# Attention of a two-layer decoder step: the low halves of four query weights are made by an adding transfer instead of a VectorE subtraction

## The chip, the cores and the metric

The kernel runs on one core of a Trainium2 chip. The time is device microseconds of the whole program, from one execution to the next the median of several runs. The profile is one execution taken by the hardware profiler; its engines are PE (TensorE, its matmuls) and PEld (its weight loads), DVE (VectorE), ACT (ScalarE), POOL (GpSimd) and SP (SyncE, which here only issues transfers).

## The reference, cut to what matters

One step of a decoder with two layers, all in float32: 512 new prompt positions and 8 sample rows (one new token each), model width 1024. Layer 0 mixes with sliding-window attention (16 query heads, 2 key/value heads, head size 64, window 128), layer 1 with gated linear attention; after each comes a ConvFFN of width 2816. The change touches only the first product of layer 0:

```python
qkv = x @ w_qkv + b_qkv                       # (520 x 1024) @ (1024 x 1280)
q, k = rope(q, pos), rope(k, pos)
scores = einsum('bnqkgd,bnskd->bnkgqs', qb, kk) * 64 ** -0.5
probs = sink_softmax(scores, mask, sink)      # softmax with one more logit per head
o = einsum('bnkgqs,bnskd->bnqkgd', probs, vv)
x = layer_norm(ALPHA * x + o @ w_o)           # then the ConvFFN, then layer 1
```

The outputs are compared with this in float32, so the kernel keeps the precision: each operand of a product is split into a high part that TensorE reads in its fast float32 form (`fp32r`) and a low part, the remainder.

## The kernel before, in words

**Units.** All weights are cut into units of 128 output columns; a unit is one array of 128 x 1024 float32 (512 KB). Units 0 and 1 are the key and value columns, units 2 to 9 the query columns (`attn_q`, two heads each), units 10 to 17 the output projection (`out_proj`), then the ConvFFN and layer 1 follow. The 520 rows of x are two groups: a (256 rows) and b (264 rows, the samples among them). Each unit is multiplied with both groups.

**A weight's way.** `load_unit` brings a unit from HBM by SP into a tile `raw` (2 buffers). ACT copies it to `wh` with rounding to `fp32r` (line 198); then DVE takes `wl = raw - wh` (line 204). `wh` and `wl` come from a pool of `WSLOTS` = 6 slots, so units 0 to 5 are loaded at the start and unit 6 takes the slot of unit 0 when both groups are done with that, unit 7 that of unit 1, and so on. For the units of the ConvFFN (`ffn_down2`, `ffn_gate`, `ffn_value`) another way is in use, `low_by_dma`: ACT writes `-wh` into `wl` (line 209), and a transfer that POOL issues reads the unit from HBM once more and adds it to `wl` while it writes (line 210).

**A product.** `product` makes, for each of 8 blocks of 128, three matmuls into one accumulator `accp`: `wh` by the high part of x (line 240), `wh` by its low part (242), `wl` by the high part (244). So 24 matmuls for a unit and a group, of which the third needs `wl`.

**Attention behind it.** `attn_q` takes each query product of a unit and a group as one task (16 of them): ACT reads `accp` (line 573, tile `ra`), DVE and POOL rotate it (575, 576, 577, 579, tile `rr`), ACT and DVE split it (624, 625, tile `hl`), SP moves the halves into place with 4 small transfers (629, tile `qs`); then come scores on PE (657 and 658, tile `sc`, in two halves of 4 matmuls), mask, maximum and exponential on DVE and ACT (667 to 677, the exponential is line 674), transposes on PE (686, tile `tp`), their copies on ACT (688) with POOL's two selections (692), and the products with the values on PE (705).

**What sets the order.** The program is written in one sequence, and a scheduler of the framework then orders each engine's instructions by its own cost model and puts the semaphores in. Each engine works through its own list strictly in that order. An instruction that waits holds up all that stand behind it on its engine. So a change of one operation's kind can move others that are not touched in the source.

Of the kernel before, what the change touches and what calls it, by code (L numbers as in the profile page):

```python
# [45 lines left out]
WSLOTS = 6  # L46
# [56 lines left out]
class Net:  # L103
# [80 lines left out]
    def load_unit(self, u, pieces=1, late=False):  # L184
        src, nt = self.units[u][0], self.units[u][1]
        nc = self.nc
        if nt == 0:
            return self.load_rank(u)
        r = self.raw.tile([P, KD * P], F32, name="raw")
        h, l = ((self.wx if u == self.extra else self.wts).tile([P, KD * P], F32R, name=name) for name in ("wh", "wl"))  # L190
        n = nt * P // pieces
        for c in (slice(i * n, (i + 1) * n) for i in range(pieces)):
            nc.sync.dma_start(out=r[:, c], in_=src[:, c])
            if late:
                self.spawn(self.parts(u, h[:, c], l[:, c], r[:, c], src[:, c]), 1)
                continue
            if u >= HIACT:
                nc.scalar.activation(h[:, c], r[:, c], AF.Copy)  # L198
            else:
                nc.gpsimd.tensor_scalar(h[:, c], r[:, c], 1.0, 0.0, op0=ALU.mult, op1=ALU.add)  # L200
            if self.units[u][2] in (self.ffn_down2, self.ffn_gate, self.ffn_value):
                self.low_by_dma(l[:, c], h[:, c], src[:, c])
            else:
                nc.vector.tensor_tensor(l[:, c], r[:, c], h[:, c].bitcast(F32), op=ALU.subtract)  # L204
        self.w[u] = (h, l)
# [1320 lines left out]
```

## Time and profile before

| | |
|---|---|
| median of 3 runs | 1097.23 us (1093.21 to 1097.97) |
| the profiled execution | 1098.08 us, of which 1096.1 us are the profile's span |
| granted TensorE clock, mean | 0.994 |
| PE matmuls busy | 1058.4 us, 97% of the span |
| DVE, ACT, POOL busy | 79%, 63%, 30% of the span |
| DMA | 167.44 MB, 153 GB/s on average |
| transfers by `low_by_dma` | 85 in the span, none of them issued before 153 us |

All times within the profile are in us from the start of the span. The attention of layer 0 lies between about 15 and 136 us; the profiled execution is 0.85 us above the median of the runs.

### The profile page before, as it was taken

To read this page: it belongs to the slowest core of one execution; us is meant where nothing else is said; L and a number is where in the kernel's file an instruction comes from. 1 tells how busy PE (TensorE), PEld (TensorE's weight loads), DVE (VectorE), ACT (ScalarE), POOL (GpSimd) and SP (SyncE) were. 2 spreads that over 40 slices of the span, in tenths; PEclk is the share of its full clock that TensorE was granted. 3 is DMA by queue.
4 is the path that set the end of the run, shared out by engine and by line. 5 is a ranking of instruction groups with operands and counts; after the bars stand their busy time and mean duration, and the time that the engine had idled before them with its cause. 6 is when DMAs were issued, how large, how long until landed. Compare 5 with 4: busy or idle time off the path is not lost.

```text
span 1096.1 us, 23852 instructions
## 1 busy us (share of the span) xinstructions
PE 1058.4 (97%) x9174; PEld 1029.8 (94%) x9174; DVE 866.2 (79%) x1812; ACT 686.1 (63%) x1356; POOL 325.8 (30%) x513
## 2 busy tenths in 40 slices
PE   8999999999999999999999999999899999999995
PEld 7998799999999999999999999898899999999995
DVE  7897758987788778978766767687888788778975
ACT  5677657776656665647666756477676656665643
POOL 3476553511111110274231111363311111110263
PEclk9999999999999999999999999999999999999998
DMA  6554139597777774348134455367487777774422
GB/s 228 150 162 136 24 108 226 129 221 183 181 174 175 174 190 117 111 144 220 55 115 157 132 157 172 93 173 209 127 212 187 181 173 177 174 188 117 114 68 79
DMA packets 65473, 167.44 MB, mean 153 GB/s; under 512 B 8104, under 2 KB 28624, under 8 KB 65360
## 3 DMA queue, kind: packets, MB, share of 16 engines
q1 hardware_dynamic: 50960, 119.47, 33.6%
q0 software_dynamic: 12240, 44.57, 23.2%
q10 hardware_dynamic: 2160, 1.89, 0.5%
q8 instruction: 72, 1.18, 0.4%
q14 instruction: 41, 0.34, 0.1%
HBM read 153.24 MB, written 8.47 MB: 148 GB/s over the span
## 4 chain that ended last, share of the span: by engine, by line
PE 76%; DVE 8%; DMA 6%; ACT 4%; POOL 2%; issue 2%; SPq 1%; DVEq 0%; ACTq 0%; POOLq 0%
PE widep L312 9%; PE widep L314 9%; PE widep L313 9%; PE accp L240 8%; PE accp L242 8%; PE accp L244 7%; PE widep L937 5%; PE widep L934 5%; PE widep L936 5%; DMA raw<-in_w_up 2%; PE accp L954 2%; DMA raw<-in_w_qkv 2%; PE onep L314 1%; PE onep L313 1%; PE onep L312 1%
## 5 line engine op out<-in xcount | busy, mean ns | idle before, releaser
L317 ACT ACTIVATE wh<-raw 128x1024 fp32r<-128x1024 f32 x72 | 76.3, 1060 | 96.2 <-PE widep L937 49.9
L198 ACT ACTIVATE wh<-raw 128x1024 fp32r<-128x1024 f32 (+1 forms) x91 | 95.0, 1047 | 40.7 <-PE widep L313 12.4
L313 PE MATMUL widep<-tl,wh 128*128 128x264 f32 (+1 forms) x432 | 119.1, 276 | 0.0
L314 PE MATMUL widep<-th,wl 128*128 128x264 f32 (+1 forms) x432 | 119.1, 276 | 0.0
L312 PE MATMUL widep<-th,wh 128*128 128x264 f32 (+1 forms) x432 | 119.1, 276 | 0.0
L240 PE MATMUL accp<-xh_b,wh 128*128 128x264 f32 x400 | 112.6, 282 | 2.5 <-DVE hprod L831 2.0
L244 PE MATMUL accp<-xh_b,wl 128*128 128x264 f32 x400 | 111.7, 280 | 0.0
L210 POOL DMA_DIRECT2D wl<-in_w_down x28 | 24.3, 866 | 284.2 <-ACT wl L209 273.1
L240 PE MATMUL accp<-xs_a,wh 128*128 128x256 f32 x400 | 105.6, 283 | 2.9 <-ACT wh L198 1.9
L242 PE MATMUL accp<-xl_b,wh 128*128 128x264 f32 x384 | 106.8, 278 | 0.0
L242 PE MATMUL accp<-xs_a,wh 128*128 128x256 f32 x384 | 102.1, 282 | 0.5 <-DVE xs_a L318 0.4
L318 DVE TENSOR_TENSOR wl<-raw,wh 128x1024 fp32r<-128x1024 f32 x72 | 88.1, 1223 | 8.1 <-ACT wh L317 8.1
L209 ACT ACTIVATE wl<-wh 128x1024 fp32r<-128x1024 f32 x85 | 89.3, 1053 | 1.1
L204 DVE TENSOR_TENSOR wl<-raw,wh 128x1024 fp32r<-128x1024 f32 (+2 forms) x63 | 77.9, 1244 | 14.0 <-ACT wh L198 13.4
L312 PEld LDWEIGHTS widep<-th,wh 128*128 128x128 f32 x432 | 82.1, 190 | 0.0
L313 PEld LDWEIGHTS widep<-tl,wh 128*128 128x128 f32 x432 | 82.1, 190 | 0.0
L314 PEld LDWEIGHTS widep<-th,wl 128*128 128x128 f32 x432 | 82.1, 190 | 0.0
L858 DVE TENSOR_TENSOR merged<-widep,conv 128x528 f32<-128x528 f32 x72 | 37.4, 561 | 55.3 <-PE widep L314 55.2
L240 PEld LDWEIGHTS accp<-xs_a,wh 128*128 128x128 f32 x400 | 76.4, 194 | 4.5 <-ACT wh L198 2.5
L312 PE MATMUL widep<-xh_b,wh 128*128 128x264 f32 x288 | 79.6, 276 | 0.0
L313 PE MATMUL widep<-xl_b,wh 128*128 128x264 f32 x288 | 79.5, 276 | 0.0
L314 PE MATMUL widep<-xh_b,wl 128*128 128x264 f32 x288 | 79.5, 276 | 0.0
(426 smaller groups left out, 4048.1 us busy)
## 6 DMA issues: line engine op xcount, KB each, us to landing
raw<-in_w_up SPq DMA_DIRECT2D x88, 512.0 KB, 3.9
wl<-in_w_up POOLq DMA_DIRECT2D x52, 512.0 KB, 6.6
raw<-in_w_down SPq DMA_DIRECT2D x44, 512.0 KB, 3.6
wl<-in_w_down POOLq DMA_DIRECT2D x28, 512.0 KB, 6.4
raw<-in_w_gla SPq DMA_DIRECT2D x24, 512.0 KB, 3.5
raw<-in_w_mix_o SPq DMA_DIRECT2D x16, 512.0 KB, 4.1
qs<-hl SPq DMA_DIRECT2D x64, 64.0 KB, 2.1
sgla<-in_state_gla SPq DMA_DIRECT2D x16, 256.0 KB, 2.7
```

Source lines behind the costliest of these rows:

```text
L198: nc.scalar.activation(h[:, c], r[:, c], AF.Copy)
L204: nc.vector.tensor_tensor(l[:, c], r[:, c], h[:, c].bitcast(F32), op=ALU.subtract)
L209: self.nc.scalar.activation(l, h.bitcast(F32), AF.Copy, scale=-1.0)
L240: nc.tensor.matmul(o, h[:, ks], xh, start=k == 0, stop=False)
L242: nc.tensor.matmul(o, h[:, ks], xl, start=False, stop=False)
L244: nc.tensor.matmul(o, l[:, ks], xh, start=False, stop=not tail and k == nt - 1)
L312: self.nc.tensor.matmul(o, h[:, ks], rh, start=k == 0, stop=False)
L313: self.nc.tensor.matmul(o, h[:, ks], rl, start=False, stop=False)
L314: self.final = self.nc.tensor.matmul(o, l[:, ks], rh, start=False, stop=k == KD // 2 - 1).ins
L317: self.nc.scalar.activation(hi, src, AF.Copy)
L318: self.nc.vector.tensor_tensor(lo, src, hi.bitcast(F32), op=ALU.subtract)
L934: self.final = nc.tensor.matmul(o, l[:, ks], rh, start=False, stop=k == nk - 1).ins
```

## The change

For the query units that take over a slot (`u >= WSLOTS`: units 6, 7, 8 and 9), `wl` is made by `low_by_dma` instead of by DVE:

```diff
-            if self.units[u][2] in (self.ffn_down2, self.ffn_gate, self.ffn_value):
+            if self.units[u][2] in (self.ffn_down2, self.ffn_gate, self.ffn_value) or self.units[u][2] == self.attn_q and u >= WSLOTS:
                 self.low_by_dma(l[:, c], h[:, c], src[:, c])
             else:
                 nc.vector.tensor_tensor(l[:, c], r[:, c], h[:, c].bitcast(F32), op=ALU.subtract)
```

So 4 subtractions go from DVE; 4 copies with a factor of -1 come to ACT, 4 transfers of 512 KB are issued by POOL. The scheduler places them anew, and with them other work of the attention. Behind unit 14's first product (about 130 us in the profile before) every engine's list is the same as before, apart from the numbers of buffers.

In the lists below `wh_445`/`wl_446` is unit 6 in both kernels, `wh_159`/`wl_160` unit 2, `wh_141`/`wl_142` unit 1; `accp_732` (now `accp_734`) is unit 6 with group a, `accp_811` unit 2 with group b, `accp_650` (now `accp_651`) unit 1 with group b.

PE before, where the first of the four units is used (35 us in the profile): the last matmuls of unit 1, then unit 6 with group a, in whole.

```order
L240 MATMUL accp_650<-xh_b_90,wh_141 128x264
L242 MATMUL accp_650<-xl_b_91,wh_141 128x264
L244 MATMUL accp_650<-xh_b_90,wl_142 128x264
L240 MATMUL accp_732<-xs_a_87,wh_445 128x256
L242 MATMUL accp_732<-xs_a_87,wh_445 128x256
L244 MATMUL accp_732<-xs_a_87,wl_446 128x256
```

PE now, at the same place, and then 28 rows on (`sc_452` is the second half of a task's scores):

```order
L244 MATMUL accp_651<-xh_b_90,wl_142 128x264
L240 MATMUL accp_734<-xs_a_87,wh_445 128x256
L242 MATMUL accp_734<-xs_a_87,wh_445 128x256
L240 MATMUL accp_811<-xh_b_90,wh_159 128x264
L242 MATMUL accp_811<-xl_b_91,wh_159 128x264
L244 MATMUL accp_811<-xh_b_90,wl_160 128x264
```

```order
L240 MATMUL accp_811<-xh_b_90,wh_159 128x264
L242 MATMUL accp_811<-xl_b_91,wh_159 128x264
L244 MATMUL accp_811<-xh_b_90,wl_160 128x264
L657 MATMUL sc_452<-khi1_210,qs_367 128x256
L658 MATMUL sc_452<-klo1_212,qs_367 128x256
L657 MATMUL sc_452<-khi1_210,qs_367 128x256
L658 MATMUL sc_452<-klo1_212,qs_367 128x256
L244 MATMUL accp_734<-xs_a_87,wl_446 128x256
```

Between unit 6's first two matmuls and the first that reads its `wl` there are now 32 others: all 24 of unit 2 with group b and the two halves of a task's scores, 4 matmuls each.

POOL, from the last rotation of the keys (30 us in the profile before) on; before:

```order
L321 COPY kc_214<-rr_434 128x8
L576 TENSOR_TENSOR ra_526<-ra_526,rope_t_97 128x256
L579 TENSOR_TENSOR rr_532<-ra_526,rb_528 128x256
L576 TENSOR_TENSOR ra_594<-ra_594,rope_t_97 128x256
L579 TENSOR_TENSOR rr_600<-ra_594,rb_596 128x256
L576 TENSOR_TENSOR ra_757<-ra_757,rope_t_97 128x256
L579 TENSOR_TENSOR rr_763<-ra_757,rb_759 128x256
L692 AFFINE_SELECT pl_487<-pt_484 128x256
```

and now, with the transfers of unit 6 (`wl_446`), 7 (`wl_680`) and 8 (`wl_857`):

```order
L321 COPY kc_214<-rr_434 128x8
L210 DMA wl_446<-in_w_qkv 128x1024
L576 TENSOR_TENSOR ra_527<-ra_527,rope_t_97 128x256
L579 TENSOR_TENSOR rr_533<-ra_527,rb_529 128x256
L576 TENSOR_TENSOR ra_595<-ra_595,rope_t_97 128x256
L579 TENSOR_TENSOR rr_601<-ra_595,rb_597 128x256
L210 DMA wl_680<-in_w_qkv 128x1024
L210 DMA wl_857<-in_w_qkv 128x1024
L692 AFFINE_SELECT pl_488<-pt_485 128x256
```

Unit 6's rotation (`ra_757`, now `ra_759`) stands behind the first selections now, and each transfer is issued ahead of rotations or selections of other tasks.

ACT, from the splitting of the keys (32 us in the profile before) on; before:

```order
L591 ACTIVATE khi1_210<-rr_434 64x256
L598 DMA out_k_prompt<-rr_434 128x128
L573 ACTIVATE ra_526<-accp_501,bq_207 128x256
L573 ACTIVATE ra_594<-accp_569,bq_207 128x256
L624 ACTIVATE hl_534<-rr_532 128x256
L674 ACTIVATE pr_382,small_383<-sc_372,small_383 128x129 x2
L198 ACTIVATE wh_678<-raw_677 128x1024
```

and now (unit 7 is `wh_679`/`wl_680`):

```order
L591 ACTIVATE khi1_210<-rr_434 64x256
L598 DMA out_k_prompt<-rr_434 128x128
L209 ACTIVATE wl_446<-wh_445 128x1024
L573 ACTIVATE ra_527<-accp_502,bq_207 128x256
L573 ACTIVATE ra_595<-accp_570,bq_207 128x256
L674 ACTIVATE pr_382,small_383<-sc_372,small_383 128x129 x2
L624 ACTIVATE hl_535<-rr_533 128x256
L674 ACTIVATE pr_393,small_394<-sc_373,small_394 128x129 x2
L604 ACTIVATE ra_676<-accp_651,par_78 128x264
L198 ACTIVATE wh_679<-raw_678 128x1024
```

The copy for unit 6's `wl` stands behind the four copies of the keys, and the copy for unit 7's follows some rows later, behind the split of unit 5's task:

```order
L624 ACTIVATE hl_603<-rr_601 128x256
L209 ACTIVATE wl_680<-wh_679 128x1024
L198 ACTIVATE wh_856<-raw_855 128x1024
L674 ACTIVATE pr_461,small_462<-sc_451,small_462 128x129 x2
L209 ACTIVATE wl_857<-wh_856 128x1024
```

In PE's new list 36 of the score matmuls of line 657 (18 halves, two each) stand behind the last product of unit 9; in the old one 34 (17 halves).

## The prediction

> **What bounds the kernel now.** I read the page first, for the engine that sets the time, then busy time by stage around the four units, because the change reorders nothing behind about 130 us.
>
> ```profile
> span 1096.1 us, 23852 instructions
> PE 1058.4 (97%) x9174; PEld 1029.8 (94%) x9174; DVE 866.2 (79%) x1812; ACT 686.1 (63%) x1356; POOL 325.8 (30%) x513
> ...
> q0 software_dynamic: 12240, 44.57, 23.2%
> ```
>
> PE is busy for 97% of the span. The number of matmuls stays as it is, so the change can win only PE's idle time and lose only by adding to it. The last line is the queue of POOL's transfers, the 85 adding ones: 23.2% of 1096.1 us over 85 is an estimate of 3.0 us of all 16 DMA engines for each.
>
> ```profile
> core 0: us, PE busy (x) PEld busy (x) DVE busy (x) ACT busy (x) POOL busy (x), PEclk, DMA share, GB/s
> 35.00:52.00 17.00, 16.43 (x146) 15.68 (x145) 15.17 (x49) 10.85 (x39) 8.85 (x14) 1.00 0.46 143
> 52.00:66.00 14.00, 13.28 (x118) 11.97 (x117) 12.44 (x38) 9.10 (x31) 9.45 (x16) 1.00 0.46 120
> 66.00:83.00 17.00, 17.00 (x156) 16.68 (x156) 16.73 (x46) 13.82 (x42) 13.69 (x19) 1.00 0.56 180
> 83.00:131.00 48.00, 44.40 (x415) 38.13 (x414) 35.04 (x121) 34.56 (x138) 25.62 (x59) 1.00 0.31 86
> ```
>
> The columns to see are the first two numbers: length of the stretch and PE's busy time in it. PE idles for 0.57, 0.72 and 0.00 us while query products are left (up to 83 us), and for 3.60 us after that, when only attention and what it lets through of the output projection remain. That makes 4.89 us in all, 0.45% of the time, and it is the most that this change can win. DVE is the fullest of the other engines (15.17 of 17.00, 12.44 of 14.00, 16.73 of 17.00), ACT and POOL have room. The granted clock is full throughout.
>
> What ends PE's idle time, up to 83 us and then behind it:
>
> ```profile
> PE sc L657 <- ACT pr L674: 0.6, 2, 0.4
> PE pv L705 <- POOL pu L692: 0.3, 1, 0.3
> ...
> PE sc L657 <- ACT pr L674: 1.3, 2, 0.7
> PE tp L686 <- ACT pt L688: 0.9, 2, 0.5
> ```
>
> The subtraction of line 204 is no releaser here: PE never waits for the `wl` of these four units. So 4 subtractions off DVE shorten nothing directly; they can only let the softmax run further ahead.
>
> **The change part by part.** First, what goes.
>
> ```profile
> 31.90 1.23 DVE L204 TENSOR_TENSOR wl<-raw,wh 128x1024 fp32r<-128x1024 f32 x1 [2.28 <-ACT wh L198]
> 33.04 0.41 DVE L593 TENSOR_TENSOR klo<-rr,khi 64x256 fp32r<-64x256 f32 x1
> ...
> 39.49 1.75 DVE L204 TENSOR_TENSOR wl<-raw,wh 128x1024 fp32r<-128x1024 f32 x1
> ...
> L204 DVE TENSOR_TENSOR wl<-raw,wh x4: 1225/1299/1747, 31.9 to 53.2; 128x1024 fp32r<-128x1024 f32 x4
> ```
>
> Four subtractions of 1.23 to 1.75 us, 5.2 us by the median, leave DVE between 32 and 55 us. The first one's `wl` is there at 33.1 us.
>
> Second, what comes, and its durations from the 85 that the kernel already has:
>
> ```profile
> L209 ACT ACTIVATE wl<-wh x85: 1040/1057/1110, 152.4 to 1019.2; 128x1024 fp32r<-128x1024 f32 x85
> ...
> L210 POOL DMA_DIRECT2D wl<-in_w_up x52: 858/865/1202, 153.8 to 1020.6; - x52
> ...
> DMA to landing us min/median/max: 5.2/6.6/10.9
> ```
>
> 4 x 1.06 = 4.2 us come to ACT and 4 x 0.87 = 3.5 us to POOL; both have the room in the table above. What counts is the last line: from the issue of such a transfer to its landing it takes 5.2 to 10.9 us, where the subtraction took 1.2.
>
> Now unit 6, step by step.
>
> ```profile
> 30.80 1.06 ACT L198 ACTIVATE wh<-raw 128x1024 fp32r<-128x1024 f32 x1 [3.68 <-DMA raw<-in_w_qkv]
> ...
> 33.07 0.42 ACT L591 ACTIVATE khi<-rr 64x256 fp32r<-64x256 f32 x1
> 33.51 0.47 ACT L573 ACTIVATE ra<-accp,bq 128x256 f32<-128x256 f32 x1
> ...
> 37.39 0.42 ACT L624 ACTIVATE hl<-rr 128x256 fp32r<-128x256 f32 x1 [2.40 <-POOL rr L579]
> 37.71 0.36 ACT L674 ACTIVATE pr<-sc,small 128x129 f32<-128x129 f32 x1
> ...
> 40.98 0.43 ACT L624 ACTIVATE hl<-rr 128x256 fp32r<-128x256 f32 x1
> ```
>
> The new list puts line 209 behind the last copy of the keys, so it starts at 33.5 and ends at 34.6 us; POOL issues then, and with the median of 6.6 us `wl` lands at 41.2, with the least of 5.2 at 39.8, with the most of 10.9 at 45.5. And when does PE need it?
>
> ```profile
> 35.11 0.27 PE L240 MATMUL accp<-xs_a,wh 128*128 128x256 f32 x1
> ...
> 37.67 0.28 PE L244 MATMUL accp<-xs_a,wl 128*128 128x256 f32 x1
> ```
>
> These are the first and the last of unit 6's 24 matmuls before: 2.56 us for 23 steps, 0.111 each. In the new list 34 matmuls stand ahead of the first one with `wl`, so PE is there at 35.11 + 34 x 0.111 = 38.9. The wait is 0.9, 2.3 or 6.6 us. The DMA engines are less loaded here (0.46) than on average where such transfers run, so I take 6.0 us, between least and median: landing at 40.6, a wait of **1.7 us**. (A late buffer for scores on the way there would cost nothing more, it lies inside this wait.)
>
> Unit 7: ACT's list has its line 209 behind the split of unit 5's task (line 624, before at 40.98). ACT was idle for 2.4 us ahead of 37.39 and takes up unit 6's extra 1.06 us there, so the split stays near 41.0, line 209 ends near 42.3 and the transfer lands at 47.5 to 48.9. PE reaches unit 7's `wl` behind 22 matmuls and 2 transposes of unit 6's and 34 matmuls and a transpose more, near 40.6 + 2.9 + 4.0 = 47.5 (a transpose counted as two steps of 0.111): a wait of 0 to 1.4, I take **0.4**. Unit 8's follows it by some 2.7 us (one copy, one pair of exponentials, line 209), PE by 2.9: **0.2**. Unit 9's `wl` is needed 66 rows, over 7 us, later: nothing. After a wait at unit 6 the later transfers are the better covered, so the waits don't add up: for all four 0.9 at least, and some 7.4 at most (6.6 and 0.8).
>
> What is queued behind the new waits: on POOL the rotations of units 4 and 5 behind the first issue (34.6 to 35.4, while the row below has unit 4's start at 35.32: 0.1 us late), the first selections and unit 6's rotation behind the second and third, since the third waits for a line 209 that ends near 45. Unit 6's scores stand 205 rows behind its first `wl` in PE's new list, over 22 us later, so this is covered. If that cover went, the tasks would come late into the tail, whose price is the last term below.
>
> ```profile
> 35.32 0.88 POOL L576 TENSOR_TENSOR ra<-ra,rope_t 128x256 f32<-128x256 f32 x1 [4.54 <-DVE rb L575]
> ```
>
> The gain on the same stretch: its idle time is waits for the exponential, which fall inside the new wait or vanish as DVE is ahead, so the 0.57 us of the first stretch go: **-0.57**. The second stretch I leave as it is.
>
> The tail, 83 to 131 us:
>
> ```profile
> L657 PE MATMUL sc<-khi,qs x34: 276/282/392, 83.8 to 126.9; 128*128 128x256 f32 x34
> ```
>
> 34 of these are 17 halves of a task in 48.0 us, 2.8 us each; the new list has 18 halves behind the query products. If the tail goes by PE's work, the half has only moved and brings its share of idle time, 3.60/17 = 0.2; if it goes by the chain of softmax steps, 2.8. PE is busy for 92% there, so I take a value near the lower end, **0.5**.
>
> Sum: 1.7 + 0.4 + 0.2 - 0.57 + 0.5 = **+2.2 us**. The profiled execution (1098.08, 1.98 of it around the span) would become 1100.3; it lies 0.85 above the median of the runs, 1097.23, to which the same sum gives **1099.4**.
>
> One page speaks to the largest term. The Trainium skill, "DMA: Bandwidth & Descriptors", section "Anatomy of one DMA — SWDGE (gpsimd) path", gives 2.0 us and the bytes over 436e3 per us for a transfer from this queue: an estimate of 3.2 us for 512 KB, by which unit 6's `wl` would land at 37.8 and the sum would be -0.1. The trace's least of 85 is 5.2, so I go by the trace.
>
> **The rivals.** That the change doesn't do what it says is excluded by the lists: four transfers more on POOL, four subtractions fewer on DVE.
>
> (1) The transfers land slowly, as the slowest of the 85 (10.9 us): 6.6 at unit 6, which covers the others, and half of the tail's upper price: 6.6 - 0.57 + 1.4 = +7.4, so 1104.6; with all at its worst 7.4 - 0.57 + 2.8 = +9.6, 1106.8. For it: the four come within 16 us, at 3.0 us of all engines each, beside `raw` and `qs`. Against: a share of 0.46 before. Chance 0.15.
>
> (2) Faster: DVE's 5.2 us let the softmax get ahead, and the idle time goes. Its place is 83 to 131 us, where PE waits for exponentials; its price all 4.89 us less unit 6's least wait of 0.9, -4.0, so 1093.2. It decides once PE's idle time in the tail falls below about 1.5 us. For it: DVE at 98% from 66 to 83. Against: PE idles for nothing in just that stretch, and the new list leaves more attention in the tail. Chance 0.15.
>
> (3) The transfer is hidden anyway: a landing within 4.3 us of its issue (34.6 to 38.9) makes no wait at all, only -0.57 + 0.5: 1097.2. This is what the page's rule would give. A plain load of the same size in this kernel needs 4.7 here:
>
> ```profile
> raw<-in_w_qkv SPq DMA_DIRECT2D x7, 512.0 KB, 4.7
> ```
>
> Chance 0.1.
>
> (4) The new heads of the queues on ACT and POOL hold up the tasks, and the tail goes by its chain: +2.3 - 0.57 + 2.8 = +4.5, 1101.7. Chance 0.15.
>
> **How the numbers follow.** My forecast, 1097.5 to 1101.5, has 0.45. About 0.5%, 5.5 us, is what a measurement of this kernel can tell from no change: faster means below 1091.7, slower above 1102.7. Faster takes all idle time of rival 2 and more: 0.05. Slower takes rival 1 (0.15) and the upper third of rival 4 (0.05): 0.2. The rest, 0.75, is the same. The range goes from 1094.0, inside rival 2, to 1105.0, which holds most of rival 1; some 0.2 lie outside.
>
> **What the new profile would show.** Right: line 204 has four entries fewer; PE waits in its list for the DMA of `wl<-in_w_qkv`, 1 to 3 us, once before all, near 39 us; PE's idle time in the first stretch rises from 0.57 to about 2.5 and the later rows are later by about 2 us from there on. Landings near 6 us. In the tail an idle time of 3.6 to 4.5 us. Wrong: no wait for that DMA (then rival 3 or 2), a wait over 4 us (rival 1), or a tail longer by 2 us and more (rival 4).

## The result, and the profile after

The change makes the kernel slower: 1105.70 us (median of 6 runs, 1104.99 to 1111.46) against 1097.12 for the kernel before beside it, a ratio of 1.0101 with a 95% interval of 1.0077 to 1.0124. On a second chip it was 1105.06 against 1095.49, 1.0091 (1.0064 to 1.0118). So +8.6 and +9.6 us, where the prediction had +2.2, and the time is 0.7 us above the range's upper end, 1105.0. The profiled execution took 1105.01 us, its span is 1103.1 (before 1098.08 and 1096.1).

The page of the changed kernel, the same three rows as before:

```profile
span 1103.1 us, 23875 instructions
PE 1065.2 (97%) x9174; PEld 1036.0 (94%) x9174; DVE 867.2 (79%) x1808; ACT 688.9 (62%) x1360; POOL 321.3 (29%) x517
...
q0 software_dynamic: 12816, 46.67, 24.0%
```

The number of matmuls is unchanged, and yet PE is busy for 6.8 us more (1058.4 before), while its idle time over the whole span hardly differs (37.7 us before, 37.9 now). Busy time that grows with the same work is a sign of a slower clock. The stages of the prediction, with the same columns (PE's busy time second, the granted clock behind POOL's busy time, then the DMA share):

```profile
35.00:52.00 17.00, 14.97 (x115) 14.43 (x113) 10.70 (x37) 13.00 (x38) 8.37 (x13) 0.90 0.92 223
52.00:66.00 14.00, 13.19 (x123) 12.35 (x121) 11.58 (x37) 8.91 (x32) 10.55 (x18) 1.00 0.63 153
66.00:83.00 17.00, 16.05 (x143) 15.32 (x141) 15.26 (x41) 11.06 (x34) 11.99 (x19) 1.00 0.48 149
83.00:131.00 48.00, 42.79 (x394) 37.04 (x395) 35.01 (x113) 32.91 (x130) 24.82 (x56) 1.00 0.34 100
```

PE idles for 2.0 us in the first stretch (0.57 before), for 0.95 in the third (0.00) and for 5.2 in the last (3.6), the clock falls to 0.90 in the first, and the DMA engines are at 0.92 there (0.46). DVE has 10.70 us of work instead of 15.17 in the first stretch: it has the room that it was to get, and PE's idle time grows all the same. What ended PE's waits, between 30 and 83 us and then between 83 and 131:

```profile
PE accp L244 <- DMA wl<-in_w_qkv: 2.5, 2, 1.7
PE tp L686 <- ACT pt L688: 0.4, 1, 0.4
PE sc L657 <- ACT pr L674: 0.4, 1, 0.4
...
PE sc L657 <- ACT pr L674: 2.5, 3, 1.7
PE pv L705 <- POOL pu L692: 1.2, 2, 0.8
PE pv L705 <- DVE hl_b L318: 0.9, 1, 0.9
PE accp L240 <- ACT ra L573: 0.6, 1, 0.6
```

The wait for unit 6's `wl` is there with 1.7 us. The second one, 0.8 us at 53.05 us, is at unit 8: unit 7's `wl` landed at 48.1 us and PE read it at 49.2 without a wait, while unit 8's took 8.7 us from its issue and landed at 53.0. It is this second landing that counts behind it. The chain that ended last, followed back, goes through ACT's copy for unit 8, the issue and the transfer (start, length, what):

```profile
43.03 0.95 ACT wl L209
43.99 0.29 issue
44.28 8.73 DMA wl<-in_w_qkv
...
53.05 0.38 PE accp L244
```

In the second profile of the changed kernel (the first experiment below) it goes the same way:

```profile
43.98 8.19 DMA wl<-in_w_qkv
```

The transfers of all four units, in the answer on the tile `wl`:

```profile
L209 ACT ACTIVATE wl<-wh x4: 1057/1064/1072, 32.4 to 50.5; 128x1024 fp32r<-128x1024 f32 x4
L210 POOL DMA_DIRECT2D wl<-in_w_qkv x4: 853/889/1027, 33.8 to 51.9; - x4
...
DMA to landing us min/median/max: 5.9/6.6/8.7
```

And the clock, in windows laid on the record of the granted clock (second number PE's busy time, the clock the third from the right). The first three rows are the changed kernel around unit 6's wait, the next two follow it at 143.7 us, the last two are the kernel before, at the only such place in it:

```profile
37.89:41.30 3.41, 1.75 (x14) 1.41 (x13) 2.91 (x9) 3.41 (x10) 1.25 (x2) 1.00 0.66 144
41.30:44.71 3.41, 3.41 (x18) 3.41 (x18) 1.16 (x5) 3.38 (x11) 1.32 (x2) 0.50 0.87 230
44.71:48.13 3.42, 3.42 (x32) 3.42 (x32) 1.16 (x5) 1.33 (x6) 1.41 (x3) 1.00 1.02 241
```

```profile
140.29:143.70 3.41, 2.28 (x18) 1.99 (x18) 1.94 (x5) 1.16 (x4) 3.41 (x7) 1.00 0.00 0
143.70:147.11 3.41, 3.41 (x21) 3.17 (x22) 0.84 (x2) 0.00 (x0) 1.06 (x5) 0.50 0.00 0
```

```profile
773.36:776.77 3.41, 0.14 (x2) 0.00 (x0) 3.41 (x9) 2.92 (x5) 1.00 (x1) 1.00 0.73 135
776.77:780.18 3.41, 3.25 (x15) 3.25 (x16) 0.77 (x1) 1.24 (x2) 0.86 (x1) 0.50 0.17 14
```

Behind the stretch with the wait, PE runs for exactly 3.41 us at half clock: 18 matmuls instead of 32 in the same time. Such a period costs half its length, 1.7 us, where nothing else is waited for behind it. Inside the run the kernel before has one, the changed kernel four (from 41.3, 143.7, 201.7 and 723.9 us).

From PE's rows the two profiles can be laid beside each other by stage; a second pair was taken on one chip (the first experiment below):

| stage, by PE's first matmul of each kind | before | after | difference | half-clock periods | PE idle | second pair | half-clock periods | PE idle |
|---|---|---|---|---|---|---|---|---|
| start to the first scores | 31.67 | 30.76 | -0.91 | 0 / 0 | | 31.17 / 30.47, -0.70 | 1 / 0 | |
| to the output projection | 51.31 | 55.00 | +3.69 | 0 / 1 | 1.27 / 4.05 | 51.30 / 54.84, +3.54 | 0 / 1 | 1.11 / 4.08 |
| to line 349 (the tail) | 44.39 | 47.41 | +3.02 | 0 / 0 | 2.88 / 4.92 | 44.20 / 48.08, +3.88 | 0 / 0 | 2.70 / 5.60 |
| to the ConvFFN's `onep` | 89.21 | 91.99 | +2.78 | 0 / 2 | 5.80 / 6.10 | 89.43 / 90.79, +1.36 | 1 / 1 | 5.12 / 5.90 |
| to the end of the span | 879.5 | 877.9 | -1.6 | 1 / 1 | | 879.6 / 876.9, -2.7 | 1 / 2 | |
| sum | | | +7.0 | | | +5.4 | | |

Three things in it were not in the sum: the clock (three periods more in the first pair, one in the second), a tail longer by 3 to 4 us where the sum had 0.5, and a part that is given back late. The last is one row, PE's wait for a transfer of the ConvFFN, first before and then after:

```profile
776.93 0.58 PE L244 MATMUL accp<-xs_a,wl 128*128 128x256 f32 x1 [3.43 <-DMA wl<-in_w_up]
```

```profile
785.44 0.38 PE L244 MATMUL accp<-xs_a,wl 128*128 128x256 f32 x1 [0.86 <-DMA wl<-in_w_up]
```

PE comes there 11.1 us later, waits 2.6 us less and goes on 8.5 us later. So the loss in the attention is larger than the loss of the whole.

### The profile page after: what moved, and what is told of

The parts are those of the page before. It is cut to its first block, busy times and chain, and to the rows that moved or that the text cites. A ratio compares the mean times of both kernels' runs of the same rounds, so it can differ in the third digit from the quotient of the medians.

```text
span 1103.1 us, 23875 instructions
## 1 busy us (share of the span) xinstructions
PE 1065.2 (97%) x9174; PEld 1036.0 (94%) x9174; DVE 867.2 (79%) x1808; ACT 688.9 (62%) x1360; POOL 321.3 (29%) x517
## 4 chain that ended last, share of the span: by engine, by line
PE 76%; DVE 9%; DMA 5%; ACT 5%; issue 2%; POOL 1%; SPq 0%; DVEq 0%; ACTq 0%; POOLq 0%
PE widep L312 9%; PE widep L313 9%; PE widep L314 9%; PE accp L240 8%; PE accp L242 8%; PE accp L244 7%; PE widep L937 5%; PE widep L934 5%; PE widep L936 5%; DMA raw<-in_w_up 2%; PE accp L954 2%; PE onep L313 1%; PE onep L314 1%; PE onep L312 1%; DVE x_b L442 1%
## 5 line engine op out<-in xcount | busy, mean ns | idle before, releaser
L209 ACT ACTIVATE wl<-wh 128x1024 fp32r<-128x1024 f32 x89 | 93.6, 1055 | 1.1
L204 DVE TENSOR_TENSOR wl<-raw,wh 128x1024 fp32r<-128x1024 f32 (+2 forms) x59 | 73.8, 1260 | 10.9 <-ACT wh L198 10.7
L240 PEld LDWEIGHTS accp<-xh_b,wh 128*128 128x128 f32 x400 | 76.4, 191 | 4.5 <-DVE hprod L831 3.2
```

The lines of the kernel that those rows point to most:

```text
L209: self.nc.scalar.activation(l, h.bitcast(F32), AF.Copy, scale=-1.0)
L240: nc.tensor.matmul(o, h[:, ks], xh, start=k == 0, stop=False)
```

## The experiments

Two theories and a third: A, the wait for the late `wl` has the predicted size and the granted clock makes the rest; B, the moved order and the queue heads on ACT and POOL lengthen the tail; C, the added transfers slow down the others on the DMA engines. Intervals are 95%, each ratio is against the kernel before on the same chip.

**The pair again.** No edit.

> The kernel before once more, for a profile of it on the same chip as the next three. All theories: the same time as before. Theory A: in each profile so far a period of 3.41 us at half clock follows a stretch of the same 3.41 us grid in which TensorE idled for 1.1 us or more; windows with less than 0.5 us idle are never followed by one. The same here, and one or two such periods before the end.

> The changed kernel once more, on the same chip as the kernel before, with its profile. The first comparison gave +8.6 us by the medians. Theory A (clock alone beside the predicted 2.2 us): at the start of the output projection's last stage (the first reduction of line 349, 127.4 us in the first profile of before, 133.2 now) it is later than before by about 2.2 plus 1.7 for each half-clock period up to there; all in all 7 to 9. Theory B (tail): free of half-clock periods it is still later by 4 to 5, of which 2.5 to 3 arise between the first matmul of the output projection and line 349.

Measured: before 1.0000 (0.9982 to 1.0019); after 1.0091 (1.0064 to 1.0118), 1105.06 us. The table above has the profiles. Theory A's figure for line 349 fails: counted from the first scores the changed kernel is 7.4 us later there, 5.7 without its half-clock period, where A has 2.2. The mean granted clock of the runs is 0.9927 before (23 runs) and 0.9903 after (6 runs): 0.0024 of 1100 is 2.6 us. So the clock is about a quarter of the loss on average at most. In the second pair's profiles PE is busy for 2.6 us more and idle for 2.8 us more; in the first pair's it was 6.8 and 0.2.

**The transfers left out.** Line 210 doesn't run for units 6 to 9, so their `wl` stays at `-wh` and the outputs are not those of the reference:

```diff
-                self.low_by_dma(l[:, c], h[:, c], src[:, c])
+                if self.units[u][2] == self.attn_q:
+                    nc.scalar.activation(l[:, c], h[:, c].bitcast(F32), AF.Copy, scale=-1.0)
+                else:
+                    self.low_by_dma(l[:, c], h[:, c], src[:, c])
```

> The changed kernel without line 210 for units 6 to 9: wl stays at -wh (the raw - part is left out), so DVE is relieved and ACT has its 4 copies more, but nothing lands late and the DMA engines carry 2 MB less. Theory A and C (the waits for the landing, the load on the DMA engines, and the clock behind them are the loss): 1096 to 1098, the time of before. Theory B (ACT's copies and the order of the tail's tasks): most of the loss stays, 1101 to 1104, with TensorE's idle time in the tail near 5 us instead of 3.6 (here 68 score matmuls stand behind the last query product as before, so 2 us of it at most).

Measured: 0.9993 (0.9977 to 1.0009), 1094.82 us. Its first and last stretch:

```profile
35.00:52.00 17.00, 17.00 (x156) 16.70 (x156) 15.07 (x50) 16.07 (x50) 9.93 (x17) 1.00 0.45 131
...
83.00:131.00 48.00, 43.98 (x397) 37.09 (x396) 34.02 (x117) 34.17 (x136) 25.44 (x58) 1.00 0.22 59
```

PE has no idle time at all in the first, with ACT at 16.07 of 17.00. Without the transfers the whole loss is gone; ACT's 4.2 us by themselves cost nothing. And it bounds the gain: with the transfers made free, the relief of DVE brings at most 0.23% in the order that this kernel got.

**POOL's wait without a landing.** In place of the transfer POOL copies two columns of `wl` (which stays at `-wh` again), and so has to wait for ACT's line 209:

```diff
+                    nc.scalar.activation(l[:, c], h[:, c].bitcast(F32), AF.Copy, scale=-1.0)
+                    nc.gpsimd.tensor_copy(self.ap.tile([P, 2], F32, name="look", bufs=4), l[:, :2].bitcast(F32))
```

> As the kernel without the transfers (wl of units 6 to 9 stays at -wh, the raw - part is left out), but in the place of each transfer POOL copies two columns of wl, so that POOL waits for ACT's line 209 as it does ahead of line 210 in the changed kernel (7.4 us in three waits there, with rotations and selections behind them). Theory P (POOL's wait at the head of its queue delays the tasks, and so makes TensorE's idle time of 5 us instead of 2.8 in the tail): 1099 to 1103. Theory L (only the late landing at TensorE, 1.7 us at unit 6 and what the displaced tasks make of it): 1094 to 1097, as without the transfers.

Measured: 0.9967 (0.9947 to 0.9987), 1093.00 us, faster than before. POOL did wait (its line in the waits from 30 to 83 us; the changed kernel's 7.4 us there below it):

```profile
POOL look L204 <- ACT wl L203: 4.9, 2, 2.6
```

```profile
POOL wl L210 <- ACT wl L209: 7.4, 3, 3.2
```

Theory P's 1099 to 1103 fails. But the test is weaker than it looks: with the operations themselves POOL is held for 5.9 us here (4.9 and 1.0) and for 12 in the changed kernel (8.3 of waits and 3.7), so it is shown only that the first half costs nothing. The order is another one again, so the 3.4 us are no pure gain of the relief.

**The transfer without ACT's copy.** POOL writes the unit itself to `wl`, so nothing is added and `-wh` is left out:

```diff
+                    nc.gpsimd.dma_start(out=l[:, c], in_=src[:, c])
```

> The changed kernel without line 209 for units 6 to 9: POOL's transfer writes the unit itself to wl without adding (the -wh part is left out). No copy on ACT and no wait of POOL for it; the transfers are issued some microseconds earlier, and TensorE's list keeps unit 6's first product whole. Theory P: ACT and POOL are free of the added work, so no loss: 1095 to 1098, if the transfer lands within its earlier issue's lead. Theory L: what counts is whether TensorE waits for wl: for each wait of 1 to 2 us in its list the time is 1.5 to 3 us over 1096; without any, 1096.

Measured: 1.0016 (0.9996 to 1.0036), 1096.90 us. Nothing has to be copied first, so the transfers are issued from 26.3 us on instead of 33.8, and land 4.0 to 6.0 us later; PE has no wait for `wl` in its list (0.34 us of idle time from the first scores to the output projection). The same 2 MB in the same queue, as plain transfers, cost nothing that can be told from noise when they start 7 us earlier.

**Transfers that nobody waits for.** The kernel before, with four more on POOL's queue:

```diff
+                if self.units[u][2] == self.attn_q and u >= WSLOTS:
+                    nc.gpsimd.dma_start(out=self.dram.tile([P, KD * P], F32, name="spare", bufs=4)[:, c], in_=h[:, c].bitcast(F32))
```

> The kernel before, DVE's subtractions kept, and beside them four further transfers of 512 KB on POOL's queue at the places where the changed kernel issues its own: each writes a unit's wh to a scratch array in HBM, and nobody waits for it. TensorE's first product with unit 6 stays whole. Theory of the late result (the loss comes from TensorE's list being built for a wl that lands earlier than it does): 1095 to 1097.5, as before. Theory of contention (transfers on the DMA engines, and their issue on POOL, delay the others): 1100 to 1104.

Measured: 1.0003 (0.9983 to 1.0022), 1097.07 us, with the DMA engines at 0.71 in the first stretch:

```profile
35.00:52.00 17.00, 16.55 (x145) 15.67 (x144) 15.30 (x47) 10.66 (x38) 9.30 (x16) 1.00 0.71 243
```

So four more transfers by themselves cost nothing. They write to HBM and add nothing, and the share is 0.71 against 0.92 with the adding ones, so that load is not reproduced in full. A second sign against contention comes from the changed kernel itself: PE does not wait for the small moves of the query products there, and these land as fast as before. From issue to landing between 30 and 95 us, before and then in the changed kernel:

```profile
DMA to landing us min/median/max: 1.9/2.8/4.8
DMA to landing us min/median/max: 1.9/2.7/5.5
```

**Unit 6 alone, and units 7 to 9 alone.** The condition of line 201:

```diff
+            if self.units[u][2] in (self.ffn_down2, self.ffn_gate, self.ffn_value) or u == 6:
```

and `7 <= u <= 9` in the other.

> Unit 6 alone gets its wl by an adding transfer; units 7, 8 and 9 subtract on DVE as before. TensorE's list again has unit 6's first two matmuls, then 32 others, then the first that reads wl, and 34 matmuls of line 657 behind the last query product as before (36 in the changed kernel). Theory A (the wait is as small as I predicted, but an idle time of 1 us or more brings periods of 3.41 us at half the granted clock, 1.7 us each): a wait of about 1.7 us for the DMA of wl near 40.7 us and a half-clock period behind it; the tail (83 to 131 us) as before. Time about 1097.1 + 1.7 + 1.7 = 1100.5, and each further period in the profile adds 1.7. Theory B (the reordered tail is the cost: one more half task and the queue heads of units 7 to 9): the tail is as before, so 1097.1 + 1.7 = 1098.8 with the clock of before. Theory C (contention of the transfers on the DMA engines): a quarter of the loss, 1099.2, and a landing of 6 us or less.

> Units 7, 8 and 9 by adding transfers, unit 6 subtracted on DVE as before. TensorE's list has no deferred unit 6 and 34 matmuls of line 657 behind the last query product. Theory A: no wait of 1.7 us near 40 us and no half-clock period there; a smaller wait (0.5 to 1 us) for unit 7's wl near 44 us can remain; time 1097 to 1099.5, and what it has over 1097.1 is the waits plus 1.7 for each half-clock period more than before's one. Theory B (queue heads in the tail): most of the loss stays, since three of the four moved copies and transfers stay: 1101 to 1104. Theory C: three quarters of the loss, 1103.5.

Measured: unit 6 alone 1.0011 (0.9991 to 1.0031), 1097.69 us; units 7 to 9 1.0044 (1.0024 to 1.0064), 1101.39. PE's wait in the one and in the other:

```profile
PE accp L244 <- DMA wl<-in_w_qkv: 1.7, 1, 1.7
```

```profile
PE accp L244 <- DMA wl<-in_w_qkv: 2.9, 2, 2.7
```

With unit 6 alone the wait is the changed kernel's, 1.7 us, yet no half-clock period follows. The stretches of its own 3.41 us grid show why: the wait lies across two of them and leaves about 1 us of idle time in each.

```profile
35.90:39.31 3.41, 2.45 (x18) 1.92 (x16) 3.21 (x11) 3.32 (x13) 2.17 (x3) 1.00 0.84 173
39.31:42.72 3.41, 2.40 (x21) 2.40 (x22) 3.41 (x9) 1.95 (x5) 0.00 (x0) 1.00 0.45 114
42.72:46.13 3.41, 3.41 (x33) 3.41 (x33) 2.62 (x10) 2.78 (x13) 2.41 (x5) 1.00 0.78 268
```

With units 7 to 9 it is unit 7 that waits, at 45 us and for 2.7 us; I had expected 0.5 to 1. In that profile a half-clock period follows (48.3 us). Theory A's upper end, 1099.5, fails there; B's 1101 to 1104 holds 1101.39, but its reason does not: PE's idle time in the tail is 3.2 us, near the 2.9 of the kernel before. For unit 6 alone no theory is told from another: its interval, -1.0 to +3.4 us, holds the forecasts of all three.

**The wait filled with work.** Superfluous matmuls right ahead of the first one that reads unit 6's `wl`:

```diff
-                nc.tensor.matmul(scs[v][:, b], qb, self.khi[v][:, keys], start=True, stop=False)
-                nc.tensor.matmul(scs[v][:, b], qb, self.klo[v][:, keys], start=False, stop=True)
+                for _ in range(1 + 7 * (g.i == 0 and u == 3 and v == b == 1)):
+                    nc.tensor.matmul(scs[v][:, b], qb, self.khi[v][:, keys], start=True, stop=False)
+                    nc.tensor.matmul(scs[v][:, b], qb, self.klo[v][:, keys], start=False, stop=True)
```

> The changed kernel with 14 superfluous matmuls (the last two score matmuls of unit 3's task, line 657 and 658, repeated seven times with the same result, 1.6 us) right ahead of the first matmul that reads unit 6's wl. They fill the wait of 1.7 us and so shift nothing behind it by more than 0.3 us. Theory that an idle time in a stretch of the clock's grid halves the clock for the next 3.41 us: no idle time above 0.3 us near 40 us, and full clock from 41 to 45 us, where both profiles of the changed kernel show half; the product of unit 6 is done 1.7 us earlier by that. Theory that the half clock there is by chance or comes from the load: it can still appear. The time: 1103 to 1105, since 62 to 68 score matmuls stand in the tail now.

Measured: 1.0090 (1.0058 to 1.0121), 1107.78 us. Windows on its own grid, and the one wait for `wl`:

```profile
36.93:40.34 3.41, 3.32 (x27) 2.96 (x25) 2.88 (x9) 3.41 (x10) 1.55 (x2) 1.00 0.80 184
40.34:43.75 3.41, 3.38 (x30) 3.38 (x31) 1.58 (x6) 3.41 (x9) 1.01 (x2) 1.00 0.91 224
...
47.33 0.38 PE L244 MATMUL accp<-xs_a,wl 128*128 128x256 f32 x1 [2.09 <-DMA wl<-in_w_qkv]
```

No idle time near 40 us and full clock behind it, as expected. But nothing was won: PE came to unit 7's `wl` at 45.2 us and waited 2.1 us for it, where the changed kernel came at 49.2 and did not wait, and it waited 3.0 us more for a selection of POOL. The first `wl` of unit 8 was read at 54.0 us, in the changed kernel at 53.05. So the wait at unit 6 and the half clock behind it were covered there by the later landings. I had missed the time by 3 us.

**Unit 6 later in the program.** Its product with group a behind unit 3's with group b:

```diff
+        out.remove((0, WSLOTS))
+        out.insert(out.index((1, 3)) + 1, (0, WSLOTS))
         return out
```

> The changed kernel with unit 6's product with group a written two products later (behind unit 3 with group b); all four adding transfers stay. In TensorE's list the first matmul with unit 6's wl comes 26 rows later, 2.9 us, more than the wait of 1.7 us. The tail has 34 matmuls of line 657 instead of 36. Theory A: the wait of 1.7 us near 40 us and the half-clock period behind it are gone, 3.4 us less than the changed kernel: about 1102 or lower, 1097 to 1099 if the two other periods (144 and 202 us) also go with the shift. Theory B: 2.8 us less at most from one half task fewer in the tail, the queue heads stay: 1103. Theory C: the transfers are all there, 1105.

Measured: 1.0075 (1.0046 to 1.0103), 1105.59 us. The wait near 40 us and the half clock behind it are gone, as theory A had it, but its times fail, the 1102 as well as the 1097 to 1099; theory C's 1105 is near. PE waits again, 2.2 us in two waits for `wl`, now at 47.7 and 53.7 us, 1.4 at a transpose, and five half-clock periods stand in the profile. The tail has 68 score matmuls as before, and yet PE idles in it for 5.6 us.

**A third buffer for `hl`,** in the changed kernel and in the one before:

```diff
-        hl = self.ap.tile([P, 2, 256], F32R, name="hl", bufs=2)
+        hl = self.ap.tile([P, 2, 256], F32R, name="hl", bufs=3)
```

> The changed kernel with three buffers for hl (the split query product) instead of two. TensorE's list is that of the changed kernel up to 66 us, so the wait of 1.7 us for unit 6's wl stays; behind the last query product there are 68 score matmuls again instead of 72. In the changed kernel's tail ACT waited 2.1 and 3.0 us (two profiles) ahead of line 624 for the transfers that read hl, and TensorE 1.7 and 2.6 us for the exponential behind it. If that is what makes the tail long: this wait goes, the idle time of the tail falls from 4.9 and 5.6 us to about 3, and the time to 1101 to 1103. If the tail is long because each task is late by itself: no gain, 1105, and the wait turns up at another buffer.

> The kernel before with three buffers for hl. TensorE idles for 2.7 to 2.9 us in its tail, of which 1.3 to 1.9 us end with an exponential. If the buffer of hl holds the tail in both kernels: 1 to 2 us faster, 1094. If not: 1095 to 1096, no change.

Measured: 1.0074 (1.0048 to 1.0101), 1105.87 us, and 1.0031 (1.0007 to 1.0055), 1099.93. With 68 score matmuls in the tail its idle time falls to 3.0 us, as expected, but the idle time ahead of it rises from 4.1 to 6.7:

```profile
PE accp L244 <- DMA wl<-in_w_qkv: 4.4, 3, 2.1
```

The buffer isn't the cause of the loss. In the kernel before, a third buffer makes things slightly worse; why wasn't followed up.

**The same exchange where there is slack,** for units 10 to 13 of the output projection (`10 <= u <= 13` in line 201), **and POOL as the subtractor:**

```diff
+                    nc.gpsimd.tensor_tensor(l[:, c], r[:, c], h[:, c].bitcast(F32), op=ALU.subtract)
```

> The same exchange (DVE's subtraction against ACT's copy and an adding transfer) for the first four units of the output projection, 10 to 13, instead of the query units 6 to 9. TensorE's list is unchanged up to 55 us, and these units are multiplied from about 78 us on, so the landing has slack. Theory A: no new wait for wl, so no new half-clock period by it: 1096 to 1098, with the clock of before. Theory B: ACT and POOL get the same 4.2 and 3.5 us of work nearer to the tail, so 1099 to 1103. Theory C: the same four transfers within some 16 us: 1105.

> The subtraction of units 6 to 9 on POOL instead of DVE: no copy on ACT, no transfer. DVE is relieved as in the changed kernel. Theory A and C: no wait for a landing near 40 us; if POOL takes 1.5 to 2.5 us for one, 1096 to 1099. Theory B in its form that any operation put ahead of the rotations and selections on POOL delays the tasks: 1099 to 1103, with TensorE's idle time in the tail above 4 us.

Measured: 1.0059 (1.0038 to 1.0079), 1101.69 us, and 1.0088 (1.0066 to 1.0110), 1105.70. Both miss theory A; theory B's 1099 to 1103 holds the first time, and the second is above it. For units 10 to 13, the waits in the tail, the stretch of their transfers, and SP's issue of one task's four small ones:

```profile
PE sc L657 <- DMA qs<-hl: 3.7, 1, 3.7
```

```profile
66.00:83.00 17.00, 17.00 (x156) 16.70 (x155) 12.41 (x43) 15.25 (x42) 12.94 (x22) 1.00 0.96 245
...
77.60 6.62 SPq L629 DMA_DIRECT2D qs<-hl  x4
```

Nobody waits for `wl`, but with the DMA engines at 0.96 the issue of the four moves of a query product takes 6.62 us (2.42 to 2.79 for four in the kernel before, 60 to 95 us), and PE waits 3.7 us for them. This is theory C, in another place. POOL's subtraction takes long itself:

```profile
L203 POOL TENSOR_TENSOR wl<-raw,wh x4: 2359/2375/2417, 30.9 to 58.9; 128x1024 fp32r<-128x1024 f32 x4
```

PE never waits for `wl` there. It waits 5.3 us for exponentials and 2.2 for selections up to 83 us: the four subtractions hold POOL for 9.5 us, ahead of rotations and selections. So a POOL held for this long costs as much as the whole change, without any transfer, which is theory B in the form that the expectation gave it.

All of them in one table. Idle is PE's, from the first scores to line 349, in the kernel's own profile:

| kernel | ratio | idle, us |
|---|---|---|
| POOL's wait without a landing | 0.9967 | 3.2 |
| transfers left out | 0.9993 | 3.2 |
| transfer without ACT's copy | 1.0016 | 3.5 |
| before (two profiles) | 1 | 4.2, 3.8 |
| before, third `hl` | 1.0031 | 4.8 |
| unit 6 alone | 1.0011 | 5.1 |
| transfers that nobody waits for | 1.0003 | 5.4 |
| units 7 to 9 alone | 1.0044 | 6.8 |
| units 10 to 13 instead | 1.0059 | 7.1 |
| wait filled (1.6 us of the busy time superfluous) | 1.0090 | 8.0 |
| changed kernel (two profiles) | 1.0101, 1.0091 | 9.0, 9.7 |
| changed, third `hl` | 1.0074 | 9.8 |
| changed, unit 6 later | 1.0075 | 11.2 |
| POOL subtracts | 1.0088 | 11.3 |

The kernels with all four adding transfers at the query units (from "wait filled" on, without the last row) idle for 8 to 11 us whatever was done to one of the waits; the time went to the next one. Idle time here is not the whole of the loss: the rows do not fall in the order of the ratios, and the profiles of the changed kernel with a third `hl` and of the transfer without ACT's copy are of their slowest runs (1110.77 and 1102.85 us).

## Why the prediction was wrong, point by point

**What was right.** The list was read rightly: the first wait is at unit 6, at 1.7 us (1.7 predicted), PE's need at 39.0 us (38.9). That the landing came at 40.6 us as predicted is luck in part: the issue was at 33.8 us instead of 34.6 and the transfer took 6.9 us instead of 6.0. The later waits were placed wrongly: none at unit 7 (0.4 predicted), since PE came there late, behind the half-clock period, and 0.8 at unit 8 (0.2), whose transfer took 8.7 us. The transfer's price by the trace held, 6.6 us in the median; the least of the four is 5.9. The estimate of 3.2 us from the Trainium skill ("DMA: Bandwidth & Descriptors", "Anatomy of one DMA — SWDGE (gpsimd) path") is not borne out by any of them. ACT's added copies and the issue of four transfers are covered by themselves, as the run without transfers and the one with idle transfers show.

**The step that failed first: the tail's term.** "I take a value near the lower end, 0.5", because PE is busy for 92% there. Measured are 3.0 and 3.9 us: 2.0 and 2.9 of idle time and about 1.0 for the half task that moved into it. The upper end, 2.8 us for a half task by its chain, had the right size, but its reason is not borne out: with unit 6 later no half task moved, and the tail idles for 5.6 us, and the chain above leads to unit 8's landing. So the step that failed is that the tail was priced by the one task that moved into it; late tasks behind the waits were not in the sum. A busy share of 92% says that PE has 8% of idle time, not that work added to the stage costs only PE's share of it.

**The gain of 0.57 us.** It was to come from a DVE that is ahead. DVE got its room, but PE's waits for the tasks did not go: apart from `wl`, 0.8 us up to 83 us, against 0.9 before. That the tasks hang on PE's products, which waited, is argued. Idle time up to the output projection rose by 2.8 and 3.0 us where waits less gain had made 1.7.

**The term that wasn't there: the clock.** "The granted clock is full throughout" was read from the profile before and carried over to a kernel with a new wait in it. The same holds for "lose only by adding to it", which meant PE's idle time: in the first pair nearly all of the loss is busy time. Three more half-clock periods would be 5.1 us of the first pair's 7.0, one more 1.7 us of the second's 5.4; over the runs it is some 2.6 us. Not all of this adds: the period at 41.3 us ends ahead of PE's wait at unit 8, so without it that wait would have been longer.

**What hid part of it.** The wait at 773 us gives 2.6 us back (3.5 in the second pair, where it is gone); no step looked behind 131 us, since no list changes there.

**The rivals.** (1) came to 1104.6, close to the time, by a landing that didn't happen (10.9 us; the slowest was 8.7). (4) named the tail's chain and had a price of the right size for it. Its cause, the heads of ACT's and POOL's queues, is not excluded in full: 5.9 us on POOL cost nothing, 9.5 us of subtractions on POOL cost 9.6 us, and the changed kernel holds POOL for 12. What speaks against it is the chain, which passes ACT's copies and the transfer. (2), the gain from DVE's relief, is bounded by the two runs without transfers at 0 to 0.5%; it needs a `wl` in time, which this change takes away. (3) was excluded by the wait.

**What stays open.** That the loss comes with the four adding transfers is shown: without them it is gone, four transfers that nobody waits for cost nothing, and in both profiles of the changed kernel the chain passes unit 8's landing. How much of it is the landing, and how much POOL's waits and issues ahead of the rotations and selections or the new order itself, is open: unit 6 alone waits for 1.7 us with a loss of 1.2 (-1.0 to 3.4), and units 7 to 9 lose 4.8 us with waits of 2.9 and a half-clock period behind them. Why 2.5 us of waits for `wl` become 5 to 6 us more of idle time is argued only: the order was made for a `wl` that comes earlier than it does, so every task behind is late against its place. The changed order with an early landing was not tried, since the scheduler orders anew with each edit. No version beat both kernels with the whole computation in it.

## What to carry to other kernels

Before moving work to a longer path, compare the path's latency with the lead that the consumer leaves: 1.2 us on an engine became 6.6 in a transfer, and the order left some 5 between its issue (33.8 us) and PE's need (39.0). Leave the operation out altogether once and time that: here it shows that at most 0.5% was to be won. And price a new wait of PE at its length, the disorder behind it, and half a clock period if it falls into one stretch of the clock's grid, not at its length alone.

## What the runs showed of the hardware

The granted clock goes by a fixed grid. In 14 of the 16 profiles (all but POOL's wait and the transfer without the copy) every half-clock period within the run is 3.413 us long or a multiple, and the distances between periods in a profile are whole multiples of 3.413 us too, wherever the waits lie. Worked out from PE's rows on each profile's grid (4291 stretches between 13 and 1060 us): of 39 stretches with 1.5 us or more of idle time 32 are followed by a period at half clock, of 219 with 0.5 to 1.5 us 17, of 4033 with less 2. So the same wait may cost 1.7 us more or not, by where it falls. The Trainium skill ("TensorE: Matmul & The Clock Gate", "Part 1: The HAM clock gate") states a free-running window of 3413 ns, which these records agree with; the rule of no idle gaps above some 3.4 us, in the same part, is too lenient here, since single gaps of 1.0 to 1.7 us were enough in the changed kernel.

A loaded DMA system slows the issue as well as the landing: four small transfers that take SP 2.4 to 2.8 us to issue in the kernel before (60 to 95 us) took 6.62 us with the DMA engines at 0.96, and from issue to landing such a transfer took 6.0 us in the median of that stretch against 2.9.
